# Gate Silus behind the attended heads, rotary keys behind two normed key heads, column sums one product group later

## The chip, the cores and the metric

The kernel runs on one core of a Trainium2 chip. A core has five engines, each with an instruction order of its own that is fixed before the run: TensorE (PE, matmuls and transposes; its weight loads are listed as PEld), VectorE (DVE), ScalarE (ACT), GpSimd (POOL), and SyncE (SP), which issues most of the DMAs. An engine takes its instructions strictly in order; one that waits for another engine's result holds up all that stand behind it. The metric is device time in microseconds, as the median of several runs.

## The reference

One block of a streaming encoder, on 512 tokens of width 1024, all in float32, with a modulation (shift, scale, gate) computed from a vector c:

```python
h = _modulate(x, sh1, s1)
x = x + 0.5 * g1[:, None, :] * _swiglu(h, ffn1_w_in[l], ffn1_w_out[l])
h = _modulate(x, sh2, s2)
y = _hybrid_mixer(h, cos, sin, w_in[l], ...)
x = x + g2[:, None, :] * y
h = _modulate(x, sh3, s3)
x = x + 0.5 * g3[:, None, :] * _swiglu(h, ffn2_w_in[l], ffn2_w_out[l])
```

`_modulate` normalises each token by its mean square over the 1024 features, scales and shifts. The mixer has two groups of four heads. Group A is a gated delta rule: q, k and v pass a short causal convolution and a Silu; a triangular system is solved in each chunk of 64 tokens; a state runs through the chunks; and the result `o_a` is normalised per head and gated:

```python
o_a = _rms(o_a, gdn_norm_w) * jax.nn.silu(gz.reshape(B, S, GDN_HEADS, GDN_DV))
```

Group B is attention over low-rank q and kv. Each of its keys has a part per head (`k_nope`, normed per head) and a rotary part that the heads share (`k_rope`); a score is the sum of the two products. Its output `o_b` is normalised per head. Both groups' heads are concatenated and multiplied by `w_out`.

## The kernel before

Data lie feature-major: a tile holds 128 features by 512 tokens. A float32 matmul is made of three matmuls of rounded parts, `mm3` (L265 to L269): high x high, high x low, low x high. A weight tile is 128 columns wide ("unit"), loaded by a DMA, its high part copied by ACT (L193) and its low part subtracted by DVE (L198).

The order of work. The kernel's Python code writes instructions in a program order, and a planner then sets each engine's order: it runs the program against prices of instructions, and at every moment takes for an engine the oldest instruction that is ready. Where the code wants an order it adds an edge: `follow` (L128) puts one instruction behind another on the same engine without a semaphore, `matmuls_in_order` (L144) makes all of PE's instructions of a stretch keep program order, and `table` (L166) chains all Exp and Silu activations on ACT, through the name in `self.tabled`, so that they keep program order and the activation table is loaded seldom. Copies, Squares and Identities are not in that chain.

The stages that the change touches:

- *Norms.* `down` and the mixer's end leave the sum of squares of each token in a tile `na`. `norm_half` (a generator) makes column sums of it on PE (`colsum`, L536, four short matmuls), the mean on DVE (L542, `ve`), the power -1/2 on POOL (L179), two diagonal tiles on DVE (L434, `dg`), spreads them with PE (L442), and then writes the modulated h in high and low parts, hh (ACT, L462) and hl (DVE, L454), by way of a tile hm or tm (DVE, L460). It yields between these steps. The two halves of the tokens are normed one after the other: while the second half is normed, `first_units` already multiplies the first half, in product groups of three matmuls numbered from 0 (`at`). At the group numbers in `marks` it takes one step of the second half's norm; the first of them issues the column sums. It is called by the mixer (`latents`, L1246, `lead` 1: group k is unit 0 with h tile k) and by FFN 2 (`ffn2`, L735, `lead` 2: groups 2k and 2k + 1 are units 0 and 1 with h tile k).

- *Keys of the attention.* `prep_k` (L1842) norms the rotary keys and rotates them on DVE (L1889 to L1893, and the copy L1859, tile `kro`), sums the squares of the four key heads (ACT L1863, DVE L1864), takes the root of their means on DVE (`rms_cols`, L182 to L189), turns the rotary keys token-major to feature-major on PE (L1869, four transposes) with a copy on ACT (L1871, tile `krT`), scales the key heads on DVE (`kn`, L1229), and turns these head by head on PE (`head_tiles`, L1783) with a scaling copy on ACT (L1785, `nT`).

- *Attention.* `attend` (L1895) makes scores (L1905 with nT, L1908 with krT), masks and maxima on DVE (L1912, L1914), Exps on ACT (through `table`), transposes (L1925) with copies (L1929, `pT`), the products with the values (L1935, tile pb), Squares of them (ACT L1939, `hn`) and copies (L1948, `ao`). Two heads share one PSUM tile. `attended` (L1959) scales a finished head on DVE (`on`), turns it (L1966) and writes its high part on ACT (L1971, `mh`) and its low part on DVE (L1972).

- *Gates.* The mixer's last four dense units are the gates z: `z_done` (L1986) copies each out of PSUM (L1988), and after the units `silu(self.zT)` (L2048) runs four Silus, tile z in place, through `table`. `gated_out` (L1739) reads z on DVE (L1760).

- *Around the gates.* The delta rule's triangular inverse runs as a side task: `inverse` (L1557) in short PE steps with copies on ACT and DVE (L1573, L1579, L1586, L1594, copies `ti` L1598, L1605, L1608, L1615, copies `T` L1616), `join` (L1620: L1636, L1639, copies `Y` L1651), `solve` and `recur`. While it runs, PE also has the dense products of the attended heads with `w_out`, `out_attended` (L2105, tiles mh and ml).

The sides are stepped from the dense loop (`dense_units` with `Rates`) and then by the loop behind the gates; the generator `others` there finishes the attention, if it has steps left, and then hands `out_attended` to the filler.

Of the kernel before, what the change touches and what calls it, by code (L numbers as in the profile page):

```python
# [14 lines left out]
AF = mybir.ActivationFunctionType  # L15
# [3 lines left out]
P = 128  # L19
# [3 lines left out]
NB = NT // P  # L23
# [56 lines left out]
class Block:  # L80
# [651 lines left out]

    def ffn2(self, nb):
        with self.tc.tile_pool(name="ws", bufs=1) as self.ws:
            ps = self.first_units(3, nb, 2, (7, 18, 15))  # L735
            with self.in_order():
                self.ffn2_rest(ps)

# [500 lines left out]
    def latents(self, nb):  # L1239

        nc = self.nc
        wq = self.up_weight("mla_w_uq", self.vcol["mla_q_norm_w"], 3, 384)
        wkv = self.up_weight("mla_w_ukv", self.vcol["mla_kv_norm_w"], 2, 512)
        next(wq)
        next(wkv)
        ps = self.first_units(3, nb, 1, (6, 15, 14))  # L1246

        def gather(ps):
            parts, acc = [], None
            for p in ps:  # L1250
                parts.append(self.split(p, "lat"))
                sq = self.slot(s="lsq")
                nc.scalar.activation(sq, p, AF.Square)
                if acc is None:
                    acc = sq
                else:
                    nc.vector.tensor_tensor(out=acc, in0=acc, in1=sq, op=ALU.add)
            return parts, acc

        pk = self.proj(self.aux())  # L1260
        qp, acc = gather(ps)
        ps = [pk]
        lq = qp, self.rms_cols(self.colsum(acc), NB, 384)
        p = self.proj()
        s = self.slot(s="kab")
        nc.scalar.copy(s[:72, :], p[:72, :])
        wq = next(wq)
        ps.append(self.proj())
        kp, acc = gather(ps)
        lkv = kp, self.rms_cols(self.colsum(acc), NB, 256)  # L1270
        wkv = next(wkv)
        return lq, wq, lkv, wkv, s
# [569 lines left out]
    def prep_k(self, kn):  # L1842

        nc = self.nc
        sk_n = self.const([P, 16], s="skn")
        kr = self.kab[:, :288].rearrange("p (b c) -> p b c", b=NB)[:, :, :64]
        s = self.slot(s="krq")
        sv = s[:, :256].rearrange("p (b c) -> p b c", b=NB)
        nc.scalar.activation(sv, kr, AF.Square)
        ss = self.small(4, "krs")  # L1850
        nc.vector.tensor_reduce(out=ss, in_=sv, axis=AX.X, op=ALU.add)
        rr = self.rms_cols(ss, 4, 64)
        kx = self.slot(s="krx")
        xv = kx[:, :256].rearrange("p (b c) -> p b c", b=NB)
        self.mul(xv, kr, self.bc(rr, 4, 64))
        ko = self.slot(s="kro")
        ov = ko.rearrange("p (b e c) -> p b e c", b=NB, e=2)
        self.rope(ov[:, :, 0, :], xv, self.rope_c["k"], self.rope_s["k"])
        nc.vector.tensor_copy(ov[:, :, 1, :], ov[:, :, 0, :])  # L1859
        yield  # L1860
        for b in range(NB):
            s = self.slot(s="akk")
            nc.scalar.activation(s, kn[b], AF.Square)  # L1863
            nc.vector.tensor_reduce(out=sk_n[:, 4 * b:4 * b + 4], in_=s.rearrange("p (h d) -> p h d", h=4), axis=AX.X,  # L1864
                                    op=ALU.add)
        rkn = self.rms_cols(sk_n, 16, 128)
        pt = self.aux()
        for b in range(NB):
            nc.tensor.transpose(pt[:, b * P:(b + 1) * P], ko[:, b * P:(b + 1) * P], self.ident)  # L1869
        self.krT = self.slot(s="krT")  # L1870
        nc.scalar.copy(self.krT, pt)  # L1871
        yield
        for b in range(NB):
            kv = kn[b].rearrange("p (h d) -> p h d", h=4)
            self.mul(kv, kv, self.bc(rkn[:, 4 * b:4 * b + 4], 4))
        yield
        jk = self.vcol["qkn_k_nope"]
        for h in range(4):
            self.knT.append(self.head_tiles([kn[b][:, h * P:(h + 1) * P] for b in range(NB)], self.cwT[:, jk:jk + 1]))
            yield  # L1880

    def rope(self, out, x, c, s):
# [76 lines left out]
    def attended(self, h, r):  # L1959


        nc = self.nc
        on = self.head_scale(self.ao[h], r)
        pt = self.aux()
        for i in range(NB):
            nc.tensor.transpose(pt[:, i * P:(i + 1) * P], on[:, i * P:(i + 1) * P], self.ident)  # L1966
        yield
        j = self.vcol["mla_out_norm_w"]
        gain = self.cwT[:, j:j + 1]
        mh, ml = self.mixed[4 + h] = self.slot(F32R, "mh"), self.slot(F32R, "ml")  # L1970
        nc.scalar.activation(mh, pt, AF.Copy, scale=gain)  # L1971
        nc.vector.scalar_tensor_tensor(out=ml, in0=pt, scalar=gain, in1=mh.bitcast(F32), op0=ALU.mult, op1=ALU.subtract)  # L1972


    def mixer(self, nb):
        nc, tc = self.nc, self.tc
# [19 lines left out]
        def silu(tiles):  # L1996
            for t in tiles:
                self.table(t, t, AF.Silu)
# [46 lines left out]

        chain.add(solving())
        self.dense_units(4, Rates(sides, (1, 0.75, 2)), 1, z_done)
        silu(self.zT)  # L2048
        accum = self.slot(s="na")

        fill = Side()
# [1 line left out]
        def others():  # L2053
            while att.open or att.todo:
                att.step()
                yield
            fill.add(self.out_attended())

        rest = Side(wide=3)
        rest.add(others())  # L2060
        while self.wk[1] is None or deltas.open or deltas.todo:
            chain.step(2)
# [112 lines left out]
```

## Time and profile before

| | us |
|---|---|
| median of the runs shown | 1050.69 (1050.64 to 1052.29, 3 runs) |
| profiled execution | 1052.1 |
| its span, first to last instruction | 1050.4 |
| PE busy | 1032.6 (98%) |
| PEld busy | 884.5 (84%) |
| DVE busy | 682.1 (65%) |
| ACT busy | 449.0 (43%) |
| POOL busy | 48.2 (5%) |
| granted TensorE clock, mean | 0.997 |

In a timeline row stand the start, the duration, the engine, the line of the kernel, the operation, what it writes and reads, the count of merged instructions, and in brackets how long the engine stood idle before it and what ended that. Matmuls overlap, so a row's duration is longer than its step to the next row: three dense matmuls over 512 tokens start 0.23 us apart, over 256 tokens 0.12 us. An ACT_TABLE_LOAD on ACT changes between the table of the Exp and that of the Silu; there are eight of them under `table` in this kernel.

### The profile page before, as it was taken

Reading aid. Unit: us, or ns where it says so; the run is one execution under the profiler, and the core shown is the slowest. Engines: PE = TensorE matmul, PEld = TensorE weight load, DVE = VectorE, ACT = ScalarE, POOL = GpSimd, SP = SyncE. Lnnn points to the kernel's source line nnn. Section 1 sums busy time; section 2 is a strip of 40 time slices with the busy share of each in tenths; the row PEclk is TensorE's granted clock in tenths of the full one; section 3 lists DMA queues with packets and bytes.
Section 4 is the critical chain, followed back from the end, with each engine's and each line's share of the span. In section 5 each row is a group of like instructions: output and inputs, shape, how many; then the busy total and the mean of one; then the engine's idle time right before and its main releaser. Section 6 shows DMA issues by size and latency. Waiting matters only on the chain.

```text
span 1050.4 us, 16101 instructions
## 1 busy us (share of the span) xinstructions
PE 1032.6 (98%) x6375; PEld 884.5 (84%) x6375; DVE 682.1 (65%) x1251; ACT 449.0 (43%) x781; POOL 48.2 (5%) x113
## 2 busy tenths in 40 slices
PE   6999999999999999999999999999999999999998
PEld 5788878788887799887777769998999999999986
DVE  4478984333486636648877556789768778777633
ACT  3342322222222226739566464465345444444422
POOL 1000000000000011100001111310000000000000
PEclk8999999999999999999999999999999999999999
DMA  9979973233586539711212201173423333333222
GB/s 275 288 224 301 303 237 101 85 96 95 184 279 220 164 99 236 179 41 51 70 42 55 72 22 41 41 162 100 136 78 102 108 101 112 92 98 105 76 61 81
DMA packets 203689, 136.88 MB, mean 130 GB/s; under 512 B 13777, under 2 KB 186590, under 8 KB 203614
## 3 DMA queue, kind: packets, MB, share of 16 engines
q1 hardware_dynamic: 202318, 131.14, 42.4%
q0 software_dynamic: 1296, 4.72, 2.4%
q8 instruction: 50, 0.82, 0.3%
q14 instruction: 25, 0.20, 0.1%
HBM read 128.63 MB, written 2.49 MB: 125 GB/s over the span
## 4 chain that ended last, share of the span: by engine, by line
PE 89%; ACT 4%; DVE 3%; DMA 1%; issue 1%; POOL 0%; SPq 0%; POOLq 0%; DVEq 0%; ACTq 0%
PE pa L267 20%; PE pa L268 20%; PE pa L269 19%; PE pb L870 6%; PE pb L869 6%; PE pb L871 6%; PE pb L268 1%; PE pb L267 1%; PE pb L269 1%; PE pb L415 1%; PE pb L1491 1%; PE pb L1905 1%; DMA xt<-in_x 1%; PE pb L1908 1%; PE pb L1935 0%
## 5 line engine op out<-in xcount | busy, mean ns | idle before, releaser
L267 PE MATMUL pa<-hh,wh 128*128 128x512 f32 (+1 forms) x565 | 216.7, 384 | 0.0
L268 PE MATMUL pa<-hl,wh 128*128 128x512 f32 (+1 forms) x565 | 214.8, 380 | 0.6 <-DVE hl L454 0.4
L269 PE MATMUL pa<-hh,wl 128*128 128x512 f32 (+1 forms) x565 | 214.6, 380 | 0.0
L193 ACT CAST wh<-wr 128x1024 fp32r<-128x1024 f32 (+1 forms) x106 | 107.8, 1018 | 247.7 <-PE pa L268 172.0
L198 DVE TENSOR_TENSOR wl<-wr,wh 128x1024 fp32r<-128x1024 f32 (+1 forms) x97 | 114.2, 1178 | 104.6 <-ACT wh L193 102.2
L267 PE MATMUL pa<-ah,wh 128*128 128x512 f32 (+1 forms) x396 | 145.6, 368 | 0.6 <-DVE xT L896 0.4
L268 PE MATMUL pa<-al,wh 128*128 128x512 f32 (+1 forms) x396 | 144.5, 365 | 0.0
L269 PE MATMUL pa<-ah,wl 128*128 128x512 f32 (+1 forms) x396 | 143.6, 363 | 0.0
L267 PEld LDWEIGHTS pa<-hh,wh 128*128 128x128 f32 x565 | 106.4, 188 | 23.1 <-issue 3.2
L269 PEld LDWEIGHTS pa<-hh,wl 128*128 128x128 f32 x565 | 106.3, 188 | 20.5 <-issue 0.9
L268 PEld LDWEIGHTS pa<-hl,wh 128*128 128x128 f32 x565 | 106.5, 188 | 19.4 <-DVE hl L454 1.0
L269 PEld LDWEIGHTS pa<-ah,wl 128*128 128x128 f32 x396 | 74.8, 189 | 12.1
L267 PEld LDWEIGHTS pa<-ah,wh 128*128 128x128 f32 x396 | 75.2, 190 | 10.3 <-ACT wh L193 1.7
L268 PEld LDWEIGHTS pa<-al,wh 128*128 128x128 f32 x396 | 75.2, 190 | 7.2
L574 DVE SCALAR_TENSOR_TENSOR aa<-ar,sc,aa 128x512 f32<-128x512 f32 x98 | 72.9, 747 | 9.5 <-DMA ar<-in_w_ada 8.3
L896 DVE SCALAR_TENSOR_TENSOR xT<-pa,mod,xT 128x512 f32<-128x512 f32 (+1 forms) x40 | 29.3, 735 | 17.6 <-PE pa L269 17.6
L869 PE MATMUL pb<-fh,wh 128*128 128x256 f32 x144 | 40.7, 283 | 0.0
L871 PE MATMUL pb<-fh,wl 128*128 128x256 f32 x144 | 40.7, 283 | 0.0
L871 PE MATMUL pb<-hh,wl 128*128 128x256 f32 x144 | 40.7, 283 | 0.0
L870 PE MATMUL pb<-fl,wh 128*128 128x256 f32 x144 | 40.7, 282 | 0.0
L870 PE MATMUL pb<-hl,wh 128*128 128x256 f32 x144 | 40.7, 282 | 0.0
L869 PE MATMUL pb<-hh,wh 128*128 128x256 f32 x144 | 40.6, 282 | 0.0
(443 smaller groups left out, 2008.4 us busy)
## 6 DMA issues: line engine op xcount, KB each, us to landing
wr<-in_ffn_w_in SPq DMA_DIRECT2D x82, 512.0 KB, 3.9
ar<-in_w_ada SPq DMA_DIRECT2D x48, 512.0 KB, 6.0
wr<-in_ffn_w_out SPq DMA_DIRECT2D x34, 512.0 KB, 3.7
ar<-in_w_ada SPq DMA_DIRECT2D x48, 256.0 KB, 4.9
wr<-in_w_in SPq DMA_DIRECT2D x21, 512.0 KB, 3.7
wr<-in_ffn_w_out SPq DMA_DIRECT2D x17, 384.0 KB, 3.4
wl<-wr POOLq DMA_DIRECT2D x9, 512.0 KB, 6.0
wr<-in_w_out SPq DMA_DIRECT2D x8, 512.0 KB, 3.7
```

Of the source, the lines that this page charges most:

```text
L193: self.nc.scalar.copy(hi, raw)
L198: self.nc.vector.tensor_tensor(out=lo, in0=raw, in1=hi.bitcast(F32), op=ALU.subtract)
L267: mm(out, wh, xh, start=start, stop=False)
L268: mm(out, wh, xl, start=False, stop=False)
L269: mm(out, wl, xh, start=False, stop=stop)
L415: nc.tensor.matmul(pg[32 * q:32 * q + 32, :256], self.sc[:, kc:kc + 1].to_broadcast([P, 32]), a[:, kc], start=(e == 0), stop=(e == 1), til ...
L574: nc.vector.scalar_tensor_tensor(out=acc, in0=a, scalar=sc, in1=acc, op0=ALU.mult, op1=ALU.add)
L869: mm(out, wh, xh, start=start and k == 0, stop=False, **kw)
L870: mm(out, wh, xl, start=False, stop=False, **kw)
L871: mm(out, wl, xh, start=False, stop=stop and k == 3, **kw)
L896: nc.vector.scalar_tensor_tensor(out=self.xT[t][:, ts], in0=p[:, ts], scalar=gate[:, t:t + 1], in1=self.xT[t][:, ts], op0=ALU.mult, op1=AL ...
L1491: nc.tensor.matmul(pa[:, ps], kh[:, ps], x[:, ps], start=True, stop=True)
```

## The change

Three places are edited. None adds or removes a computation.

1. The four gate Silus are no longer written right behind the gates' dense units. They are written in `others`, once the attention has no steps left, and they are made to follow the last high-part Copy of an attended head on ACT: `attended` keeps that Copy's name in `self.ended`, and the chain of `table` is set to it.
2. In `prep_k` the four transposes of the rotary keys, their PSUM tile and the copy krT move from in front of the scaling of the key heads to behind the second key head's transposes and copy.
3. The first mark of `first_units` is one higher, in the mixer (6 to 7) and in FFN 2 (7 to 8).

```diff
     def ffn2(self, nb):
-            ps = self.first_units(3, nb, 2, (7, 18, 15))
+            ps = self.first_units(3, nb, 2, (8, 18, 15))
...
     def latents(self, nb):
-        ps = self.first_units(3, nb, 1, (6, 15, 14))
+        ps = self.first_units(3, nb, 1, (7, 15, 14))
...
     def prep_k(self, kn):
         rkn = self.rms_cols(sk_n, 16, 128)
-        pt = self.aux()
-        for b in range(NB):
-            nc.tensor.transpose(pt[:, b * P:(b + 1) * P], ko[:, b * P:(b + 1) * P], self.ident)
-        self.krT = self.slot(s="krT")
-        nc.scalar.copy(self.krT, pt)
         yield
...
         for h in range(4):
             self.knT.append(self.head_tiles([kn[b][:, h * P:(h + 1) * P] for b in range(NB)], self.cwT[:, jk:jk + 1]))
+            if h == 1:
+                pt = self.aux()
+                for b in range(NB):
+                    nc.tensor.transpose(pt[:, b * P:(b + 1) * P], ko[:, b * P:(b + 1) * P], self.ident)
+                self.krT = self.slot(s="krT")
+                nc.scalar.copy(self.krT, pt)
             yield
...
     def attended(self, h, r):
-        nc.scalar.activation(mh, pt, AF.Copy, scale=gain)
+        self.ended = nc.scalar.activation(mh, pt, AF.Copy, scale=gain).ins.name
...
     def mixer(self, nb):
         self.dense_units(4, Rates(sides, (1, 0.75, 2)), 1, z_done)
-        silu(self.zT)
         accum = self.slot(s="na")
...
             while att.open or att.todo:
                 att.step()
                 yield
+            self.tabled = self.ended
+            silu(self.zT)
             fill.add(self.out_attended())
```

## The prediction

> **What bounds the kernel now.** I read the head of the page first, then TensorE's waits, then the busy time of the two stretches in which the change lies, and last the order of time around each wait.
>
> ```profile
> span 1050.4 us, 16101 instructions
> PE 1032.6 (98%) x6375; PEld 884.5 (84%) x6375; DVE 682.1 (65%) x1251; ACT 449.0 (43%) x781; POOL 48.2 (5%) x113
> ```
>
> PE has work for 98% of the span: 1050.4 - 1032.6 leaves 17.8 us without any. The change neither adds nor removes a matmul, so what it can give is time in which PE stands still, or lose is more of it. The waits of PE, named by what ended them (columns: total us, times, longest):
>
> ```profile
> PE pb L1966 <- DVE on L1229: 1.5, 1, 1.5
> ...
> PE pb L1869 <- DVE kro L1859: 0.8, 1, 0.8
> PE pb L1925 <- ACT pr L168: 0.5, 1, 0.5
> PE pb L536 <- DVE na L478: 0.5, 2, 0.3
> ...
> PE pb L1935 <- ACT ao L1948: 0.4, 1, 0.4
> PE pa L268 <- DVE hl L454: 0.4, 1, 0.4
> ```
>
> Five of these lie next to the change: L1966 (transposes of the last two attended heads) and L1935 just before it, L1869 (transposes of the rotary keys), L536 (column sums of both norms) and L268 behind one of them. Together 1.5 + 0.4 + 0.8 + 0.5 + 0.4 = 3.6 us, 0.34% of the span. That is the size of the whole question. Two stretches by busy time (columns: stretch, length, then busy us of PE, PEld, DVE, ACT, POOL):
>
> ```profile
> 504.00:520.00 16.00, 15.21 (x70) 12.35 (x69) 15.54 (x46) 6.01 (x10) 0.09 (x1) 1.00 0.35 93
> ...
> 610.20:616.10 5.90, 5.56 (x28) 4.09 (x26) 1.04 (x4) 5.78 (x14) 0.91 (x3) 1.00 0.00 0
> ```
>
> In the first, DVE is full (15.54 of 16.00); in the second, ACT is (5.78 of 5.90). So the rotary-key wait belongs to a full DVE and the attended-head wait to a full ACT.
>
> **Part 1: the gate Silus.** Before, they and their table load stand in ACT's order in front of what the last attended heads need:
>
> ```profile
> 609.60 0.58 ACT L1929 COPY pT<-pb 128x512 f32<-128x512 f32 x1
> 610.19 1.28 ACT L168 ACT_TABLE_LOAD   x1
> 611.49 0.63 ACT L168 ACTIVATE z<-z 128x512 f32<-128x512 f32 x1
> 612.02 0.25 ACT L1948 COPY ao<-pb 128x128 f32<-128x128 f32 x1
> ...
> 614.07 0.63 ACT L168 ACTIVATE z<-z 128x512 f32<-128x512 f32 x1
> 614.61 0.36 ACT L1939 ACTIVATE hn<-pb 128x256 f32<-128x256 f32 x1
> ...
> 615.01 1.16 ACT L168 ACTIVATE z<-z 128x512 f32<-128x512 f32 x2
> ...
> 619.87 0.69 ACT L1971 ACTIVATE mh<-pb,cwT 128x512 fp32r<-128x512 f32 x1
> 620.58 0.81 ACT L1598 COPY ti<-pb 32x128 f32<-32x128 f32 x3
> 622.46 0.37 ACT L1616 COPY T<-pb 64x256 f32<-64x256 f32 x1 [1.07 <-PE pb L1615]
> ...
> 624.77 0.36 ACT L1616 COPY T<-pb 64x256 f32<-64x256 f32 x1 [0.40 <-PE pb L1615]
> ```
>
> ```profile
> 612.32 1.16 PE L1935 MATMUL pb<-vn,pT 128*128 128x128 f32 x8
> ...
> 617.33 0.63 PE L1966 MATMUL pb<-ident,on 128*128 128x128 f32 x4 [1.53 <-DVE on L1229]
> ...
> 625.33 0.73 PE L1636 MATMUL pb<-T,at 64*64 64x64 f32 x9
> ```
>
> The block is 612.02 - 610.19 = 1.83 us for the load and the first Silu, so one Silu takes 1.83 - 1.30 = 0.53 in a row, and all of it is 1.30 + 4 x 0.53 = 3.42. What goes: the copy ao at 612.02, for which L1935 waits 0.4, and the squares hn at 614.61, though their matmuls end by 612.32 + 1.16 = 613.48. That is 1.13 late on ACT. What stays: hn to L1966 is 617.33 - 614.61 = 2.72, through two small DVE steps, POOL's power and the scaling; nothing of the change shortens it:
>
> ```profile
> 615.76 0.70 POOL L179 TENSOR_TENSOR roots<-va,mhalf 128x2 f32<-128x2 f32 x1 [4.66 <-DVE va L1946]
> 616.50 1.29 DVE L1229 TENSOR_TENSOR on<-ao,roots 128x512 f32<-128x512 f32 x2 [0.88 <-POOL roots L179]
> ```
>
> So of 1.53 + 0.4 = 1.93 us, 1.13 + 0.4 = 1.53 depends on the Silus and 0.4 does not. The planner orders PE anew, though: it now holds the heads for earlier, can put L1966 in front of some of the dense matmuls that it set ahead of it, and the 2.72 then stand open again. Bounds: 0 (all given back) and 1.9 (all gone). I take **1.1**, the 1.53 less the 0.4 that stays.
>
> Where the block goes: behind the last attended Copy, which ends at 619.87 + 0.69 = 620.56. Queued behind it on ACT are the three ti copies at 620.58 and the four T copies from 622.46. The ti copies are older in program order and ready, so I let them go first, until 621.39; then the block ends at 621.39 + 3.42 = 624.81, and the four T copies, packed some 0.3 apart, at about 626.0 rather than 625.13. Their reader L1636 begins at 625.33, on the first T; the first T would be there at 625.2. The 1.1 us of above pulls all of this forward, and PE can take dense matmuls of the attended heads' output (out_attended) meanwhile. Cost between 0 and 3.42 (the block wholly on the path of the inverse, which then bounds the stage); nearest is L1636's own row, 0.2 behind the T copies: I take **0.2**. The Silus' first reader is far off:
>
> ```profile
> L1760 DVE SCALAR_TENSOR_TENSOR mf<-pb,cwT,z x16: 340/343/351, 648.4 to 676.3; 128x128 f32<-128x128 f32 x16
> ```
>
> 648.4 is 23 us after 625, so the gates themselves cost nothing. The number of table loads stays: the Exps of the heads are over before 610.19 already.
>
> The Trainium skill prices the load higher ("ScalarE: Activation LUTs", What ACT_TABLE_LOAD costs): 1283 ns and a drain of 1380 ns, 2.66 us a switch. The rows disagree here: pT ends at 610.18, the load starts at 610.19 and the first Silu at 611.49, 1.31 us in all, with no room for a drain. By that rule the block would be 4.80 us, and its cost behind the heads 1.4 more; I go by the rows.
>
> **Part 2: the rotary keys.** PE waits 0.79 for kro at 508.51; its four transposes move behind those of two normed key heads:
>
> ```profile
> 508.51 0.63 PE L1869 MATMUL pb<-ident,kro 128*128 128x128 f32 x4 [0.79 <-DVE kro L1859]
> ```
>
> ```profile
> 520.00 2.50 DVE L1229 TENSOR_TENSOR kn<-kn,ry 128x512 f32<-128x512 f32 x4
> ```
>
> ```profile
> 520.84 1.16 PE L1783 MATMUL pb<-ident,kn 128*128 128x128 f32 x8
> ```
>
> ```profile
> 523.17 2.42 ACT L1785 ACTIVATE nT<-pb,cwT 128x512 f32<-128x512 f32 x4 [1.21 <-PE pb L1783]
> ```
>
> By then kro is 12 us old, so that wait is gone. Next late is kn: DVE, full since 504, ends the first of its four products at 520.00 + 0.63 = 520.63, and PE takes the first transposes at 520.84, only 0.21 behind. A PE that comes 0.79 sooner meets an unfinished kn unless more dense matmuls are set ahead of it. Bounds 0.2 and 0.8; I take **0.4**. The krT copy goes between the second and third of the four copies nT, 0.6 each (2.42 / 4). The two heads behind it come that much later, and the first scores with krT wait for it; dense matmuls of the value heads stand there to cover it: 0. Without that cover 0.6.
>
> **Part 3: the column sums.** One group of three matmuls later at each norm.
>
> ```profile
> 405.78 0.52 PEld L536 LDWEIGHTS pb<-ones,na 128*128 128x128 f32 x4 [0.34 <-issue]
> ```
>
> ```profile
> 694.32 0.61 PE L536 MATMUL pb<-ones,na 128*128 128x1 f32 x4 [0.33 <-DVE na L478]
> 694.79 0.36 PE L267 MATMUL pa<-hh,wh 128*128 128x256 f32 x1
> 695.58 0.39 PE L268 MATMUL pa<-hl,wh 128*128 128x256 f32 x1 [0.42 <-DVE hl L454]
> 695.80 0.28 PE L269 MATMUL pa<-hh,wl 128*128 128x256 f32 x1
> ```
>
> ```profile
> 694.97 0.16 DVE L542 TENSOR_SCALAR ve<-pb 128x2 f32<-128x2 f32 x1 [0.30 <-PE pb L536]
> 695.04 0.48 DVE L454 SCALAR_TENSOR_TENSOR hl<-tm,mod,hh 128x256 fp32r<-128x256 f32 x1
> ```
>
> At the mixer's norm a ready group (0.36 us) takes the place of a wait of 0.34: **0.3** won, bounds 0 and 0.34, and the sums come no later. At FFN 2's the group that goes ahead is the very one that waits for hl at 695.58. Before, hl stood on DVE behind ve, and ve waits for the sums; after, ve comes behind it, so hl can start when DVE comes free, some 0.35 sooner (0.30 idle and ve), and end near 695.15. Then PE does L268, L269 and the sums (0.47 from 694.32 to 694.79) by about 695.9, where it is today. One wait has only swapped places: **0**, bounds +0.7 (0.33 + 0.42 both gone) and -0.4 (ve ahead of the next hl). No part issues a DMA or moves past SP's queue; on POOL the power of the second norm comes a group later.
>
> **The sum.** 1.1 - 0.2 + 0.4 + 0.3 + 0 = 1.6 us. The profiled execution took 1052.1, its span 1050.4; less 1.6 they are 1050.5 and 1048.8. The shown runs have a median of 1050.69, 1.4 under the profiled one, so I forecast 1050.69 - 1.6 = **1049.1**.
>
> **The rivals.**
> *All waits go and none comes back* (22%): 1.93 + 0.79 + 0.34 + 0.33 = 3.4, so 1047.3. For it: each wait is one event on PE with a named cause that the change goes at. Against it: kn only 0.21 ahead of its transposes, and the 2.72 behind hn.
> *The waits only move* (22%): PE is held by what DVE and ACT deliver, and stands as long at the next reader: 0.4 back at L1966 of 1.53, kn for kro, hl for the sums. What is left is about 0.4, so 1050.3. For it: DVE full from 504 to 520, PE close behind. Against it: ACT in the second stretch is full because of the very block that leaves.
> *The block lands on the inverse's path* (12%): the planner sets load and Silus ahead of the ti copies at 620.58, the inverse's steps come 3.42 later, and L1966, moved ahead, keeps its wait. 3.42 less 0.7 of the other parts is 2.7 more: 1053.4. It decides if the Silus stand ahead of the ti copies and PE's dense matmuls do not last; from about 1.8 us of wait in front of L1605 to L1636 the change loses. Against it: the age of the ti copies. By the price of a load in the Trainium skill (the page and section named above) this would be 1.4 more, 1054.8.
> *The forecast* (44%): 1049.1, by itself 1048.2 to 1050.2.
>
> **The numbers.** A measurement of this kernel tells about 0.2% (2.1 us) from no change. Faster by that (under 1048.6): the first rival and a third of the forecast, 0.22 + 0.15 = 0.37. Slower (over 1052.8): the last rival, 0.12. The rest, 0.51, is within. The range goes from 1046.9, a little under the first rival, to 1052.0, which takes in most of the block's unknown cost and leaves out the last rival.
>
> **What would show it.** L1869 gone from PE's waits, and whether a wait for kn stands at L1783. L1966's wait at 0.4 or less (part 1 right), or near 1.5 (given back). On ACT, load and Silus behind both mh copies, and a wait of PE at L1605, L1615 or L1636 of less than 0.5; one over 1.8 makes me wrong. L536 gone from the waits, L268 <- hl still there at FFN 2's norm. It would also be wrong if PE's order from 500 to 640 came out so different that waits appear at lines that I do not name.

## The result, and the profile after

The changed kernel took 1048.86 us (median of 13 executions, 1047.01 to 1050.96) against 1050.94 (13 executions) of the kernel before on the same chip: ratio 0.9981, 95% interval [0.9972, 0.9989], or -2.0 us. Timed once more at the end of the study, on another occasion, it took 1047.37 (6) against 1052.02 (10): 0.9964 [0.9950, 0.9979], -3.8 us (the two medians alone are 4.65 apart; the ratio is not formed from them). The forecast was 1049.1, -1.6 us. The first measurement lies just inside the 0.2% that the prediction called no change, the second outside it. The change makes the kernel faster, by about a quarter of a percent; the forecast was a little too cautious in the sum and, as the runs show, wrong in how the sum is made up.

Times of single executions vary by 4 us for a reason that has nothing to do with the change (the last section), so most of what follows is read with a ruler inside the trace: from L1102, which occurs once, at 88 us, to the first L1754 (the transposes of the first gated output), behind both the rotary keys and the attended heads. The first L1573 (the first step of the inverse) lies between them and splits the ruler: ahead of it are the mixer's norm, the rotary keys and the first two attended heads, behind it the last two attended heads and, in all kernels, the gate Silus. Start, duration, engine, line and operation of the three, first in the kernel before:

```profile
88.04 0.27 PE L1102 MATMUL pb<-ident,cw 57*128 57x57 f32 x1
...
588.91 0.45 PE L1573 MATMUL pb<-ti,at 32*32 32x32 f32 x32
...
647.74 0.63 PE L1754 MATMUL pb<-ident,on 128*128 128x128 f32 x4
```

The same three in the changed kernel:

```profile
87.06 0.27 PE L1102 MATMUL pb<-ident,cw 57*128 57x57 f32 x1
...
585.46 0.45 PE L1573 MATMUL pb<-ti,at 32*32 32x32 f32 x32
...
643.98 0.62 PE L1754 MATMUL pb<-ident,on 128*128 128x128 f32 x4
```

That is 559.70 us before and 556.92 after: **-2.78 us**, of which 58.83 - 58.52 = 0.31 lie behind L1573. Behind L1754 the two traces differ by less than 0.1 us. The head of the page after shows the same number of instructions, and a PE whose busy time fell by 3.9 us while the span fell by 3.8:

```profile
span 1046.6 us, 16101 instructions
...
PE 1028.7 (98%) x6375; PEld 882.6 (84%) x6375; DVE 682.5 (65%) x1251; ACT 448.5 (43%) x781; POOL 48.2 (5%) x113
```

So the gain doesn't show as idle time that went away: 1046.6 - 1028.7 is 17.9 us of idle, and it was 17.8. Part of both falls lies in the start-up (last section). For the rest: a dense matmul is shown with 0.39 us while the next one starts 0.23 behind it, so up to 0.16 of a gap behind it counts as busy; and matmuls that run one behind the other instead of side by side are busy as well. What is won has to be read from start to start. The waits of PE after (total us, times, longest):

```profile
PE pb L1936 <- ACT ao L1949: 0.9, 2, 0.4
...
PE pb L1783 <- DVE kn L1229: 0.4, 1, 0.4
PE pa L267 <- ACT hh L462: 0.4, 1, 0.4
...
```

(From the edit on, lines are one higher after: L1967 was L1966, L1936 was L1935, L1949 was L1948.) Against the list of before: the wait for kro is gone, L1966 fell from 1.5 to 0.4, L536 is gone, L268 still waits 0.4 for hl, and nothing waits at L1605, L1615 or L1636; new are the waits for kn and for hh, and the wait of L1936 for ao, which was 0.4 once, is now 0.9 in two places. ACT in the stage of part 1, after:

```profile
606.62 0.27 ACT L1949 COPY ao<-pb 128x128 f32<-128x128 f32 x1
...
613.29 0.69 ACT L1972 ACTIVATE mh<-pb,cwT 128x512 fp32r<-128x512 f32 x1
614.00 1.07 ACT L1598 COPY ti<-pb 32x128 f32<-32x128 f32 x4
615.09 1.28 ACT L168 ACT_TABLE_LOAD   x1
616.39 2.19 ACT L168 ACTIVATE z<-z 128x512 f32<-128x512 f32 x4
618.60 1.17 ACT L1616 COPY T<-pb 64x256 f32<-64x256 f32 x4
```

Load and Silus stand behind both mh copies and behind the ti copies, and the T copies wait for them, as the prediction had it. On PE after, in the same stage:

```profile
606.94 1.16 PE L1936 MATMUL pb<-vn,pT 128*128 128x128 f32 x8 [0.44 <-ACT ao L1949]
610.88 0.63 PE L1967 MATMUL pb<-ident,on 128*128 128x128 f32 x4 [0.37 <-DVE on L1229]
...
620.27 0.67 PE L1636 MATMUL pb<-T,at 64*64 64x64 f32 x8
```

L1636 begins 620.27 - 610.88 = 9.39 us behind L1967; before it was 625.33 - 617.33 = 8.00. The 1.39 us more are full of dense matmuls: busy time by stretch (PE, PEld, DVE, ACT, POOL, granted clock, DMA) has PE at 8.60 of 8.60:

```profile
611.60:620.20 8.60, 8.60 (x148) 5.93 (x146) 5.36 (x12) 7.99 (x18) 0.00 (x0) 1.00 0.22 63
```

### The profile page after: what moved, and what is told of

Its sections match the earlier page's. It is cut to its first block, busy times and chain, and to the rows that moved or that the text cites. A ratio compares the mean times of both kernels' runs of the same rounds, so it can differ in the third digit from the quotient of the medians.

```text
span 1046.6 us, 16101 instructions
## 1 busy us (share of the span) xinstructions
PE 1028.7 (98%) x6375; PEld 882.6 (84%) x6375; DVE 682.5 (65%) x1251; ACT 448.5 (43%) x781; POOL 48.2 (5%) x113
## 4 chain that ended last, share of the span: by engine, by line
PE 90%; DVE 3%; ACT 3%; issue 1%; DMA 1%; SPq 0%; POOL 0%; POOLq 0%; ACTq 0%; DVEq 0%
PE pa L267 20%; PE pa L268 20%; PE pa L269 20%; PE pb L869 6%; PE pb L870 6%; PE pb L871 6%; PE pb L268 1%; PE pb L267 1%; PE pb L269 1%; PE pb L415 1%; PE pb L1906 1%; DMA ar<-in_w_ada 1%; PE pb L1936 1%; PE pb L1491 1%; DVE cv L1435 1%
## 5 line engine op out<-in xcount | busy, mean ns | idle before, releaser
L267 PE MATMUL pa<-hh,wh 128*128 128x512 f32 (+1 forms) x565 | 216.8, 384 | 0.4 <-ACT hh L462 0.4
L268 PE MATMUL pa<-hl,wh 128*128 128x512 f32 (+1 forms) x565 | 214.5, 380 | 0.5 <-DVE hl L454 0.4
L267 PE MATMUL pa<-ah,wh 128*128 128x512 f32 (+1 forms) x396 | 145.5, 368 | 0.6 <-DVE xT L896 0.4
L268 PE MATMUL pa<-al,wh 128*128 128x512 f32 (+1 forms) x396 | 144.5, 365 | 0.0
L267 PEld LDWEIGHTS pa<-hh,wh 128*128 128x128 f32 x565 | 106.4, 188 | 24.0 <-issue 3.7
L268 PEld LDWEIGHTS pa<-hl,wh 128*128 128x128 f32 x565 | 106.5, 188 | 19.5 <-DVE hl L454 0.9
L267 PEld LDWEIGHTS pa<-ah,wh 128*128 128x128 f32 x396 | 75.2, 190 | 10.4 <-ACT wh L193 1.7
L268 PEld LDWEIGHTS pa<-al,wh 128*128 128x128 f32 x396 | 75.2, 190 | 7.2
```

The source lines that it names most:

```text
L267: mm(out, wh, xh, start=start, stop=False)
L268: mm(out, wh, xl, start=False, stop=False)
```

## Experiments

Each run was compared with the kernel before on its own chip. The ruler (L1102 to the first L1754, before 559.70 us) is that of one profiled execution; the last run says how far it repeats. The last column is the part of the difference that lies behind the first L1573, before 58.83 us.

| run | ratio, 95% interval | ruler, us | against before | behind L1573 |
|---|---|---|---|---|
| all three parts | 0.9981 [0.9972, 0.9989] | 556.92 | -2.78 | -0.31 |
| the same once more | 0.9964 [0.9950, 0.9979] | 557.11 | -2.59 | -0.27 |
| part 1 alone | 0.9992 [0.9978, 1.0006] | 559.29 | -0.41 | -0.31 |
| part 2 alone | 0.9982 [0.9968, 0.9996] | 557.56 | -2.14 | -0.02 |
| part 3 alone | 0.9990 [0.9976, 1.0004] | 559.12 | -0.58 | 0.00 |
| parts 2 and 3 | 0.9970 [0.9951, 0.9989] | 557.59 | -2.11 | -0.03 |
| all, Silus written later | 0.9968 [0.9951, 0.9985] | 557.07 | -2.63 | -0.26 |
| all, four more Silus | 0.9964 [0.9944, 0.9985] | 557.04 | -2.66 | -0.33 |
| part 2, keys behind head 1 | 0.9983 [0.9961, 1.0004] | 558.22 | -1.48 | +0.01 |
| part 2, keys behind head 4 | 0.9983 [0.9960, 1.0006] | 557.82 | -1.88 | +0.03 |
| all, keys behind head 3 | 0.9973 [0.9962, 0.9984] | 557.36 | -2.34 | -0.27 |
| all, ao copies together | 0.9991 [0.9978, 1.0005] | 557.51 | -2.19 | -0.31 |
| parts 2 and 3, ao together | 0.9973 [0.9956, 0.9991] | 557.40 | -2.30 | -0.52 |

The intervals overlap throughout: the times alone would tell no two of these variants apart. (The expectations below count from a dense matmul at 60 us to the end, which gives the same differences within 0.1 us.)

### Part 1 alone

```diff
-        nc.scalar.activation(mh, pt, AF.Copy, scale=gain)
+        self.ended = nc.scalar.activation(mh, pt, AF.Copy, scale=gain).ins.name
-        silu(self.zT)
         accum = self.slot(s="na")
...
+            self.tabled = self.ended
+            silu(self.zT)
             fill.add(self.out_attended())
```

> Part 1 alone: the four gate Silus behind the last attended Copy; rotary keys and column sums as before. The prediction's sum gives -0.9 us for it (1.1 won at the attended heads less 0.2 for the block of load and Silus). The rival, read from the stages of the changed kernel's trace: L1966 does lose 1.2 us of its wait there, but PE stands 0.6 longer at the matmuls of the last heads just before, so the stage gives only 0.3 and the whole kernel -0.3. In the trace: wait at L1966/L1967 0.3 to 0.5 by both; the stage from 560 to 640 us is shorter by 0.9 (prediction) or by 0.3 to 0.4 (rival).

Measured: -0.41 us by the ruler, so the rival. PE in this run (line numbers as before the change):

```profile
610.50 1.16 PE L1935 MATMUL pb<-vn,pT 128*128 128x128 f32 x8 [0.43 <-ACT ao L1948]
614.45 0.63 PE L1966 MATMUL pb<-ident,on 128*128 128x128 f32 x4 [0.37 <-DVE on L1229]
```

L1966 waits 0.37 instead of 1.53: the 1.16 that the Silus cost there are won. But the last heads' L1935, which had no wait at 612.32 before, now has one of 0.43. Before, PE had dense matmuls to do while ACT did the table load and the first Silu; the planner brings L1935 forward when load and Silus are gone, right behind the copies pT and ao, and PE meets the unfinished ao. Of the 0.41, 0.31 lie in this stage, behind L1573.

### Part 2 alone

```diff
-        pt = self.aux()
-        for b in range(NB):
-            nc.tensor.transpose(pt[:, b * P:(b + 1) * P], ko[:, b * P:(b + 1) * P], self.ident)
-        self.krT = self.slot(s="krT")
-        nc.scalar.copy(self.krT, pt)
         yield
...
+            if h == 1:
+                pt = self.aux()
+                for b in range(NB):
+                    nc.tensor.transpose(pt[:, b * P:(b + 1) * P], ko[:, b * P:(b + 1) * P], self.ident)
+                self.krT = self.slot(s="krT")
+                nc.scalar.copy(self.krT, pt)
             yield
```

> Part 2 alone: rotary keys turned behind the second normed head, the rest as before. The prediction's sum gives -0.4 us (the wait of 0.79 for kro gone, 0.4 of it back in front of the normed heads). The rival, read from the stages of the changed kernel's trace: the stretch from 413 to 568 us gives 2.0 us, more than the named wait held, since PE is ordered anew there and smaller waits go as well. So -0.4 against -2.0 in time, and in the trace the stretch from the end of the mixer norm to 568 us is shorter by 0.4 or by 2.0.

Measured: -2.14 us. Some three quarters of the whole change lie here. Counted along PE's dense matmuls, the same one comes 1.38 us earlier at 530 us and 1.9 earlier at 568. Three of the causes can be read straight off. First, the scores with the rotary keys, in the kernel before:

```profile
523.91 0.49 PE L1905 MATMUL pb<-nT,nT 128*128 128x128 f32 x2
524.33 0.48 PE L1908 MATMUL pb<-krT,qrT 64*128 64x128 f32 x2
524.74 0.50 PE L268 MATMUL pa<-hl,wh 128*128 128x512 f32 x1
525.08 0.38 PE L1905 MATMUL pb<-nT,nT 128*128 128x128 f32 x2
525.39 0.49 PE L1908 MATMUL pb<-krT,qrT 64*128 64x128 f32 x2
525.80 1.16 PE L1491 MATMUL pb<-cv 128*128 128x128 f32 x8
```

and in this run, with the head of the stage:

```profile
519.16 0.39 PE L267 MATMUL pa<-hh,wh 128*128 128x512 f32 x1
519.95 0.44 PE L1783 MATMUL pb<-ident,kn 128*128 128x128 f32 x2 [0.40 <-DVE kn L1229]
...
523.69 0.38 PE L1906 MATMUL pb<-nT,nT 128*128 128x128 f32 x2
523.83 0.48 PE L268 MATMUL pa<-hl,wh 128*128 128x512 f32 x1
524.15 0.38 PE L1906 MATMUL pb<-nT,nT 128*128 128x128 f32 x2
524.46 0.49 PE L1909 MATMUL pb<-krT,qrT 64*128 64x128 f32 x4
524.88 1.16 PE L1491 MATMUL pb<-cv 128*128 128x128 f32 x8
```

Each head's product with krT uses 64 of PE's rows, one head the upper and one the lower half. Before, krT was there first and each head's product went as soon as its own nT was there: 0.41 us for one head (524.33 to 524.74), 0.41 for the other. With krT the last of the three, both go together and take 0.42 for the two (524.46 to 524.88). The products with nT, on all 128 rows, gain too: from start to start they took 0.42 + 0.31 us before and take 0.14 + 0.31 here, 0.28 less. Second, the wait for kro: from L267 at 507.32 to L1869 at 508.51 were 1.19 us, where dense matmuls in a row stand 0.23 apart, so it cost 0.96; the new wait for kn costs 519.95 - 519.16 - 0.23 = 0.56. That is 0.40 net, the prediction's term to the digit. The third, at the first attended heads, is found in the next run.

### Part 3 alone

```diff
-            ps = self.first_units(3, nb, 2, (7, 18, 15))
+            ps = self.first_units(3, nb, 2, (8, 18, 15))
...
-        ps = self.first_units(3, nb, 1, (6, 15, 14))
+        ps = self.first_units(3, nb, 1, (7, 15, 14))
```

> Part 3 alone: the column sums of both norms one group of three matmuls later, the rest as before. The prediction's sum gives -0.3 us, all of it at the mixer norm, 0 at FFN 2's (bounds -0.4 to +0.7). The rival (parts do not add: the order of PE behind the norm comes out otherwise when the norm ends sooner) lets the stretch behind the mixer norm move by as much as part 2 did, to -1 or to +1 us. In the trace: L536 gone from PE's waits at the mixer norm, the stretch from 413 to 640 us unchanged within 0.2 (prediction) or changed by 0.5 or more (rival).

Measured: -0.58 us. The ruler's start, and the first of the two places at which it gains, in this run:

```profile
89.46 0.27 PE L1102 MATMUL pb<-ident,cw 57*128 57x57 f32 x1
...
521.95 1.17 PE L1783 MATMUL pb<-ident,kn 128*128 128x128 f32 x8
```

L1783 stands 432.49 behind L1102 here and 520.84 - 88.04 = 432.80 before: -0.31, the mixer norm, as predicted. The other 0.27 come from the first two attended heads: before, PE stood 0.27 in front of their L1966 (567.66, where the matmul ahead had started at 567.16; in a row 0.23 apart), a wait too short for the list. Here it is gone, as it is in part 2 alone; with parts 2 and 3 together it stands again. It goes back to a DMA. The delta rule sends a tile out to memory by one DMA (L1528) and brings it back as `ba` by two more (L1532); DVE's first step with it (`bw`) waits for the landing, and `on` of the attended heads stands behind that step on DVE. Before, and in this run:

```profile
563.23 0.16 DVE L1229 TENSOR_TENSOR bw<-ba,bt 128x1 f32<-128x1 f32 x1 [0.65 <-DMA ba<-a_d]
```

```profile
564.07 0.16 DVE L1229 TENSOR_TENSOR bw<-ba,bt 128x1 f32<-128x1 f32 x1 [0.39 <-DMA ba<-a_d]
```

From this step to `on` DVE stands idle in neither kernel, so the 0.26 of shorter wait are the 0.27 at L1966. From the issue of the first DMA (556.28 before, 557.38 here) to this step it is 6.95 us before and 6.69 here; in parts 2 and 3 together it is 7.10, in the two executions of the changed kernel 6.78 and 6.80, and in part 2 alone no such wait is shown. Whether an edit or the single execution makes the DMAs faster or slower is not shown, so these 0.27 can't be credited to part 3. At FFN 2's norm:

```profile
695.22 0.38 PE L267 MATMUL pa<-hh,wh 128*128 128x256 f32 x1 [0.38 <-ACT hh L462]
695.95 0.39 PE L268 MATMUL pa<-hl,wh 128*128 128x256 f32 x1 [0.34 <-DVE hl L454]
696.29 0.50 PE L536 MATMUL pb<-ones,na 128*128 128x1 f32 x4
```

L536 waits no more; L267, put in front of it, waits for hh, and L268 still waits for hl: 0.72 us of waits against 0.75 before. Neither theory holds as stated: the norms do what was predicted, and the stage of the first attended heads, 160 us behind the first of them, moves by 0.27 us.

### All parts, the Silus written later

```diff
-            self.tabled = self.ended
-            silu(self.zT)
             fill.add(self.out_attended())
...
+        self.tabled = self.ended
+        silu(self.zT)
         na = self.norm_half(0, accum, 6, True)
```

> All three parts, with the four gate Silus written one step later in the program, behind the loop that runs the inverse: on ACT the four copies T and one copy Y then stand between load, Silus and Silus instead of behind all four Silus. The prediction put 0.2 us on the block standing ahead of the T copies, so this should be 0.2 us under the changed kernel, -1.8 against before. The rival: the block is wholly covered by the dense matmuls of the attended heads' output, then this equals the changed kernel within 0.1 us in the stage, and only the table load's place differs.

Measured: -2.63 us, between the two executions of the changed kernel. The copies T now stand among the Silus, and it makes no difference that can be told: the 0.2 set against the block is not there.

### Parts 2 and 3 without part 1

```diff
-        self.ended = nc.scalar.activation(mh, pt, AF.Copy, scale=gain).ins.name
+        nc.scalar.activation(mh, pt, AF.Copy, scale=gain)
...
+        silu(self.zT)
         accum = self.slot(s="na")
...
-            self.tabled = self.ended
-            silu(self.zT)
             fill.add(self.out_attended())
```

> Parts 2 and 3 without part 1: the gate Silus stay where they were before. By the prediction's sum part 1 carries 0.9 of the 1.6 us, so this keeps only -0.7 against before. By the stages of the runs so far (from 60 us to the end: part 1 alone -0.43, part 2 alone -2.22, part 3 alone -0.57, all three -2.85) part 1 is worth next to nothing beside the others, and this keeps -2.4 to -2.8 us in the trace and some -2 in time.

Measured: -2.11 us. Without part 1, 2.11 of 2.6 to 2.8 us stay; the prediction's sum would have left 0.7. Part 1 adds 0.5 to 0.7 to the others. That is more than alone because the small wait at the first L1966, gone in part 2 alone and in part 3 alone, is back here (from 563.95 to 564.40 is 0.45, 0.22 more than in a row), and gone again with all three. In its own stage, behind L1573, part 1 adds 0.24 to 0.28 here, about the 0.31 that it gives alone; the rest lies at the first attended heads, where DVE waits 0.56 us for `ba` in this run and 0.26 to 0.27 with all three parts:

```profile
563.95 0.39 PE L268 MATMUL pa<-hl,wh 128*128 128x512 f32 x1
564.40 0.63 PE L1967 MATMUL pb<-ident,on 128*128 128x128 f32 x4
```

### The rotary keys at other heads

```diff
-            if h == 1:
+            if h == 0:
```

This is the run behind the first head; behind the fourth it is `h == 3`, behind the third `h == 2`. The first two are made on part 2 alone, the last on all three parts.

> Part 2 alone, with the rotary keys' transposes one place earlier, behind the first normed key head. If the gain of part 2 comes from the transposes standing within the transposes of the normed heads (one stretch of them on PE where there were two, and scores whose krT is not late), any place among the heads does, and this gains the 2.2 us of part 2 alone within 0.2. If it comes from the place behind the second head alone (the first two scores need two heads and krT), this comes 0.2 to 0.6 us behind it: the second head's copy nT stands behind the krT copy, and the first scores come 0.6 later.

Measured: -1.48, that is 0.66 of the 2.14 lost. The scores of this run are split again:

```profile
521.84 0.38 PE L1906 MATMUL pb<-nT,nT 128*128 128x128 f32 x2
522.15 0.49 PE L1909 MATMUL pb<-krT,qrT 64*128 64x128 f32 x2
522.57 0.49 PE L1906 MATMUL pb<-nT,nT 128*128 128x128 f32 x2
522.98 0.48 PE L1909 MATMUL pb<-krT,qrT 64*128 64x128 f32 x2
```

krT is there before the second head's nT, the first head's product goes alone, and the two take 0.42 and 0.42 us. The products with nT take 0.31 + 0.41 between them, 0.27 more than in part 2 alone. Together 0.69: the split scores are the whole loss. It was not a late copy that cost the gain, as the expectation had it, but an early one.

> Part 2 alone, with the rotary keys' transposes two places later, behind the fourth normed key head. The prediction put no price on the copy krT as long as value heads' matmuls cover the scores, and 0.6 us without that cover. Here krT is the last of five copies on ACT, 1.2 us later than in part 2: covered, the gain stays at 2.2 us; not covered, 0.6 to 1.2 us of it are lost at the first scores (L1906, L1909), where PE then shows a wait for nT or krT.

Measured: -1.88, 0.26 behind part 2 alone, and no wait at the first scores: the copy that comes 1.2 us later is covered, and the two heads' products stay together. The 0.26 are lost further on, and they are hardly more than one execution differs from the next.

> All three parts, the rotary keys' transposes behind the third normed key head instead of the second. Behind the first head part 2 lost 0.8 us of its 2.2, behind the fourth 0.4. If the loss is that of the copy krT coming late for the first scores, the third place loses 0.2 us or less; if the second place is the only one at which the scores keep together, it loses 0.4 as the fourth did.

Measured: -2.34, 0.25 to 0.44 behind all parts with the second head. Here too the scores are together. Which of the two expectations holds can't be told. Behind L1573 this run gives 0.27, as the other runs with part 1 do; what it lacks lies ahead of it.

### All parts, a longer block

```diff
             self.tabled = self.ended
+            junk = self.slot(s="zj")
+            for t in self.zT:
+                self.table(junk, t, AF.Silu)
             silu(self.zT)
```

This kernel does four Silus more than the reference asks for, into a tile that nothing reads.

> All three parts, with four more Silus (the gates into a tile that nobody reads) ahead of the four: the block on ACT grows by 4 x 0.53 = 2.1 us, and the last of the four copies T is that much later. The prediction put 0.2 us on the block of 3.42 and said that above some 1.8 us of wait in front of L1605 to L1636 the change loses. If the dense matmuls of the attended heads' output cover the block, this costs less than 0.3 us against the changed kernel, and no wait stands at L1615 or L1636; if the block is at the edge of its cover, PE waits 1 to 2 us at L1615 or L1636 and the time is that much longer.

Measured: -2.66 us, as the changed kernel. On ACT:

```profile
619.59 2.19 ACT L168 ACTIVATE z<-z 128x512 f32<-128x512 f32 x4
621.67 0.36 ACT L1616 COPY T<-pb 64x256 f32<-64x256 f32 x1
```

The last copy T begins at 621.67, where the four of the changed kernel were over by 618.60 + 1.17 = 619.77; no wait appears at L1615 or L1636. The three other copies T went in between the extra Silus, so the test is weaker than meant: it shows a cover of 2 us for one copy, not for four.

### The copy ao

```diff
-            nc.scalar.copy(self.ao[h][:, ts], po[:, e * P:(e + 1) * P])
+                for k, g2 in enumerate(heads):
+                    nc.scalar.copy(self.ao[g2][:, ts], po[:, k * P:(k + 1) * P])
             yield
```

Both copies now stand under the `if e:` of the second head.

> All three parts, and the copy ao of the first of two attended heads (ACT, L1949 of the changed kernel) written behind the matmuls of the second head instead of between them. In the changed kernel PE waits twice at L1936 for that copy (0.9 us by the page, 0.6 of it where part 1 moved the stage forward). If that wait is what takes back part 1's gain, it goes here, and the time from 60 us to the end is 0.6 to 1.2 us under that of the changed kernel (-3.5 to -4.0 against before instead of -2.85). The rival: the wait is really for pT, copied just ahead of ao on ACT, or it goes to the next reader (L1967); then this is within 0.2 us of the changed kernel.

Measured: -2.19 us; the theory that ao takes back part 1's gain, and that moving it wins that back, falls. PE's waits of this run from 540 to 620 us:

```profile
...
PE pb L1968 <- DVE bt L1546: 0.4, 1, 0.4
...
```

Both waits for ao are gone, as meant; but the first two heads' transposes now wait 0.4 for a DVE step of the other chain (bt), and the whole is 0.4 to 0.6 us longer than the changed kernel. Behind L1573 nothing is lost (-0.31, as there). The loss is the DMA of `ba` again:

```profile
561.01 0.16 DVE L1229 TENSOR_TENSOR bw<-ba,bt 128x1 f32<-128x1 f32 x1 [1.02 <-DMA ba<-a_d]
```

The first DMA, which waits for copies on ACT (bd, L1525), is issued at 554.21, 466.79 us behind L1102; in the changed kernel it is 553.03, or 465.97. It takes as long as there (6.80 us to this step), so DVE waits 1.02 instead of 0.26, and `on` comes that much later. Why the copies on ACT are later is open.

> Parts 2 and 3 with the same move of the copy ao, the gate Silus where they were before. If the copy ao took back part 1's gain, part 1 is worth its 1.1 us with the copy out of the way: this comes 1.1 us or more behind the run of all three parts with the move. If it didn't, the difference stays at the 0.75 us measured without the move (-2.85 against -2.10).

Measured: -2.30 us. With the copies together part 1 is worth nothing (-2.19 with it, -2.30 without); both expectations miss. What part 1 is worth depends on what else is in the order: 0.41 alone, 0.5 to 0.7 on parts 2 and 3, nothing here. Behind L1573, where the Silus are, it gives some 0.3 in every run that has it; this run, without it, gains 0.52 there by the copies alone, so the two edits are after the same time.

### The changed kernel once more

> The changed kernel once more, nothing edited: how well does one profiled execution tell a stage? If the time that differs between executions lies in the first 60 us alone (the granted clock is below 1.00 there, and differently each time), the stretch from 60 us to the end comes out 2.85 us under before again, within 0.1. If the later stages vary too, it differs by 0.3 or more, and none of the differences of 0.4 to 0.8 us between the runs here means anything.

```profile
86.14 0.27 PE L1102 MATMUL pb<-ident,cw 57*128 57x57 f32 x1
643.25 0.62 PE L1754 MATMUL pb<-ident,on 128*128 128x128 f32 x4
```

Measured: 557.11, 0.19 from the first execution. That is more than the 0.1 expected and less than the rival's 0.3. Behind L1573 the two executions differ by 0.04, and the six kernels with neither part 1 nor the moved copies agree within 0.06; from L1102 to the column sums of the mixer's norm (L536) all 14 traces agree within 0.06. Most of the spread thus lies between, from 406 to 589 us. So differences of 0.4 us and more (part 1 alone, the split scores, the ao copies) stand; those of 0.2 to 0.3 on the whole ruler (the keys behind the third or fourth head) don't, while 0.3 behind L1573 does. For the whole ruler one repeat of one kernel is all there is.

## Why the prediction was right, and where it was wrong

**The sum** was -1.6; the times say -2.0 and -3.8, the ruler -2.6 to -2.8. It came out near because a term that was too large and two that were too small almost cancelled; that is luck.

| term | forecast | alone, by the ruler |
|---|---|---|
| part 1, Silus | -1.1 + 0.2 | -0.41 |
| part 2, rotary keys | -0.4 | -2.14 |
| part 3, column sums | -0.3 + 0 | -0.58 |

Alone they add up to 3.13; together they gave 2.59 to 2.78, since the 0.27 in front of the first L1966 is in two of them.

**Part 1: the step that failed** is "What goes: the copy ao at 612.02, for which L1935 waits 0.4". The list of waits names lines, not places, and L1935 occurs for every pair of heads. In the kernel before, the 0.4 stood here:

```profile
556.55 0.94 PE L1935 MATMUL pb<-vn,pT 128*128 128x128 f32 x6 [0.43 <-ACT ao L1948]
```

That is another pair of heads, 55 us ahead of the Silus. The row at 612.32, quoted in the prediction, carries no wait. So 0.4 of the 1.53 could not go, and it didn't: the wait is one of the two for ao that stand after. A slip in the sum hid this: 1.53 is already without the 0.4 that stays at L1966, and the step to 1.1 takes 0.4 off once more, which leaves about the 1.13 of L1966 alone. The other step, 1.13 at L1966, was right (1.16, with 0.37 left where 0.4 were forecast). What the sum left open, that "the 2.72 then stand open again" behind hn, happened one step earlier: L1935 came forward and met the copy ao, 0.43 by its row. Won 1.16, lost at least 0.43, the rest in small changes of the order: -0.31 is left in this stage, -0.41 in all.

**The block of 3.42 us** took the place foretold: behind the mh copies, the ti copies ahead, the T copies late. Its cost of 0.2 can't be told from none. The rival that set it on the path of the inverse fell with the ti copies at 614.00, ahead of the load. The prediction also weighed the Trainium skill's price of a table switch ("ScalarE: Activation LUTs", What ACT_TABLE_LOAD costs: 1283 ns and a drain of 1380 ns). After, the load begins at 615.09 and the first Silu at 616.39: 1.30 us, again with no room for a drain.

**Part 2** was right in the mechanism that it named (kro's wait gone, 0.96 by starts; kn's there, 0.56; L1783 now in the list) and mis-sized by 1.7 us, because it priced only waits. The two heads' products with krT running together give 0.40 more, and the products with nT beside them 0.28, read off the rows above; the run that splits them again loses 0.66. That makes 1.08 of the 1.38 gained by 530 us. Of the 0.76 behind 530 us, 0.27 is the gap at L1966, where DVE no longer waits for the DMA of `ba`. The other 0.3 and 0.5 come with PE's new order, and no experiment here took them apart. They stay open.

**Part 3** was right at both norms: 0.31 for 0.3, and "one wait has only swapped places" at FFN 2's, though the wait that came is for hh on ACT and not for hl alone. The 0.27 elsewhere was not foreseen, and by the DMA rows it need not be part 3's.

**The rivals.** "The waits only move" (1050.3) describes part 1 and FFN 2's norm, and not part 2. "All waits go" (1047.3) has nearly the size of the result and not its mechanism: the waits for kn, hh and ao are there.

## What to carry to other kernels

Before a wait of the summary is put into a sum, find its row: a line that runs in a loop may wait at another place than the one that is edited. Where PE is 98% busy, idle time is not what there is to gain: read starts against starts, and look at which matmuls stand next to each other, since matmuls on half of PE's rows pay only in pairs. An edit that lets a planner order a stage anew carries gains and losses of 0.2 to 0.6 us that no single wait foretells; price them as a range, and do each part alone before believing any term. Where a wait comes and goes between variants, follow it back past the engine that is named: here a wait of PE for DVE was one of DVE for a DMA.

## What the runs showed of the hardware

**Two 64-row matmuls run side by side only when they are issued next to each other.** In the kernel before one head's product with krT took 0.41 us; side by side both took 0.42, and 0.42 each when two products of 128 rows stood between them. The Trainium skill has the rule ("TensorE: Matmul & The Clock Gate", Part 3: Packing small matmuls): matmuls on different groups of rows overlap, starting some 4 ns apart. The trace agrees where they are neighbours, and shows that an order in which each goes as soon as it can loses it.

**Executions differ by the clock of the first 30 us.** The granted clock (third number from the right) from 15 to 25 us, in the kernel before:

```profile
15.00:20.00 5.00, 4.72 (x28) 3.57 (x20) 3.41 (x9) 1.92 (x3) 0.98 (x30) 0.57 1.18 308
20.00:25.00 5.00, 5.00 (x28) 2.60 (x27) 0.43 (x1) 0.96 (x2) 0.14 (x5) 0.74 1.18 308
```

and in the second execution of the changed one:

```profile
15.00:20.00 5.00, 4.25 (x30) 2.71 (x20) 4.15 (x11) 1.92 (x3) 1.12 (x32) 1.00 1.18 308
20.00:25.00 5.00, 5.00 (x41) 3.34 (x44) 1.25 (x4) 2.00 (x4) 0.00 (x0) 1.00 1.18 309
```

From 30 us on the clock was 1.00 in all 14 traces; L1102 began between 85.54 and 89.77 us in them, although up to there all kernels do the same. In the five traces with 1.00 from 10 us on it began at 85.54 to 86.82, in the two with the lowest clock (0.50, then 0.56 and 0.58) at 89.46 and 89.77. These 4.2 us are more than anything the change does. The Trainium skill (the same page, Part 1: The HAM clock gate) says that PE runs at half its clock until it has been busy for a window of some 3.4 us, and that the windows run free of the kernel's start. A clock of 0.57 in one execution and 1.00 in the other fits that; a clock of 1.00 for the first 5 us, in which PE is busy for 0.37, does not, and no run here tested it.
